# Latent attention: exponentials left in PSUM, the key sums split in two, and the value products carried over the halves

## The chip, the cores and the metric

The program runs on one core of one Trainium2 chip. The metric is the device time of one launch in microseconds (us). TensorE (PE in the profile, PEld for its weight loads) multiplies matrices into PSUM, eight banks of 128 partitions by 512 float32 numbers. VectorE (DVE) and ScalarE (ACT) read PSUM and SBUF and write either. GpSimd (POOL) works on SBUF here. All DMAs of this kernel are issued by SyncE (SP).

## The reference, cut to what matters

Two blocks run one after the other on 1024 tokens of width 1024, all in float32. The first is a pooling mixer beside an attention with a window. The second projects its normed input into a latent attention (8 heads, the part that changes), a dilated attention (24 heads in three groups), and gates, and merges them. The latent attention is a full softmax attention over all 1024 keys:

```
q = concat(q_nope, rope(q_rope)) * 96 ** -0.5        # 96 numbers a head
k = concat(k_nope, rope(k_shared))
s = einsum('bqhd,bkhd->bhqk', q, k)
p = softmax(s, axis=-1)
out = einsum('bhqk,bkhd->bqhd', p, v)                # 64 numbers a head
y_mla = (out * silu(z_mla)) @ w_o_mla
```

## The kernel before, in words

**Products in parts.** Every float32 operand of a product is split into a leading part (hi) and a rest (lo), both of the type that TensorE takes. `sub_lo` (L114, the instruction is L115) makes the rest: lo = source - hi. A projection adds three products, hi hi, hi lo and lo hi (`mm3`, L139 to L141).

**The latent attention** (L790 to L929) runs over 8 heads, each in two halves of 512 queries, each half over 8 blocks of 128 keys. For a block, three matmuls (L886 to L888) put scores as [128 keys, 512 queries] into one of three PSUM banks; a row of ones in the keys and the negated row maximum in the queries subtract the maximum. ACT takes the exponential into SBUF (`E`, L893), ACT copies its leading part (`ph`, L896), and DVE subtracts for the rest (`pl`, L898 through L115); both of its inputs lie in SBUF. Two blocks later (`LATE`) two matmuls, L880 with `ph` and L881 with `pl`, multiply by the same weights `vm`, which hold the hi and lo columns of the values side by side, and add up in one PSUM bank `o` over the half. So `o` holds the product with the values' hi on 64 partitions and with their lo on the other 64. At the end of the half all blocks still waiting are multiplied at once (L912), ACT copies one part of `o` to SBUF (L915), DVE adds the other (L916), and the sum goes to DRAM (L917).

**The denominators.** POOL adds the exponentials of the half, pair by pair (L902) and once more at the end (L920). In the next half, after block 5 (`SUMS`), `key_sums` (L832) splits that sum into hi and lo (`eh`, `el`) and multiplies both by a column of ones; a copy (L841) and a DMA bring the row to `den_d`. `finish` (L844, at heads 2, 4 and 6 and once later) takes two heads' outputs and denominators from DRAM, divides and gates them.

**The maxima of the next head.** `row_max` (L814) makes the scores of 128 queries against half of the keys from the leading parts alone (L818, one matmul into one of two banks `psT`) and DVE reduces them (L819). A head needs 16; the list `MAXES` says how many are written after each block of the head before. `max_rows` (L821) joins them, transposes them, and sends them by two DMAs (L830) into row 96 of the next head's queries; it is written after the head's last block.

**Fillers.** Projections that nothing needs until later (`fill`, 48 matmuls each, with a weight load, a split L125 and L115, and two evacuations) are written into the heads at places that `MLA_FILL` lists: 16 of them in all.

**Order.** The code is written in program order, and a planner that simulates the engines with its own costs then fixes the order of each engine's instructions. On the chip each engine runs its list in that order, and one that waits holds all that stand behind it. The planner's costs are fixed before the run.

**Banks.** `share_banks` deals out the eight PSUM banks: in this stage two for projections, three for scores, one for `o`, two for maxima, sums and transposes.

Of the kernel before, what the change touches and what calls it, by code (L numbers as in the profile page):

```python
# [19 lines left out]
# columns of the constant input (shapes alone)  # L20
# [30 lines left out]
def turn_parts():  # L51
    """1 / (2 pi) as a sum of five numbers of 12 bits."""
    from fractions import Fraction

    rest = Fraction("0.15915494309189533576888376337251436203445964574045644874766734405889679763")
    parts = []
    for _ in range(5):
        e = 0
        while rest * 2 ** e < 2 ** 11:
            e += 1  # L60
        n = int(rest * 2 ** e)
        parts.append(n * 2.0 ** -e)
        rest -= Fraction(n, 2 ** e)
    return parts
# [3 lines left out]
def hybrid_kernel(  # L68
# [21 lines left out]
    def share_banks(p, s, o, t=2):  # L90
        """The eight banks: p for projections, s for scores, o for outputs, t for transposes."""
# [37 lines left out]
    def load_w(src, n=128, kt=KT):  # L129
        """hi and lo of src, [kt * 128, n] of DRAM, as [128, kt, n]."""  # L130
        raw = raw_w()[:, :kt, :n]
        nc.sync.dma_start(raw, src.rearrange("(k p) n -> p k n", p=128))
        return split_w(raw, kt, n)

    def mm3(ps, pairs):
        """ps = sum of lhsT.T @ rhs over ((lh, ll), (rh, rl)) pairs, three products each."""
# [9 lines left out]
    def proj_half(w, h, half, kt=KT, ps=None):  # L146
        """[128, 512] of PSUM: columns of w against half of the tokens of h."""
# [11 lines left out]
    def rstd_of(ss, n):  # L159
        """(ss / n + eps) ** -0.5 of a column or several."""  # L160
# [7 lines left out]
    def norm_T(xt, gain, H, t, ahead=False):  # L168
        """Rows of xt (128 tokens), normed, times gain, transposed into H (hi, lo)."""
# [27 lines left out]
    def V_natural(vt, v):  # L197
        """vt, [2 heads x 64, tokens], to v, [tokens of a tile, tile, head, (hi | lo), 64]."""
# [9 lines left out]
    # ------------------------------------------------------------ attention of a window  # L208
    class Head:
        """Scores of 8 query tiles in [query, key] layout, probabilities, and their product  # L210
        with the values as [value (hi | lo), query].

        tiles[i] = (k0, kw, p0): keys k0 .. k0 + kw go to columns p0 .. of query tile i;
        keys[c] = [(query tile, its columns)] of the 128 keys whose values are v(c)."""
# [35 lines left out]
        def values(self, dest):  # L250
            """dest(half, top, bottom): the output is top + bottom, [64, 512] each."""
# [57 lines left out]
    # ------------------------------------------------------------ rope tables  # L309
    cs_d = tc.dram_tile([3, 32, S], F32, name="cs_d")  # L310

    def rope_tables():
        """cos, sin and -sin of position * frequency, [frequency, token]; the angle is taken
        to turns with 1 / (2 pi) in parts of 12 bits, so that each product is exact."""
# [40 lines left out]
    # ------------------------------------------------------------ first block  # L355
# [8 lines left out]
    def silu2(w, H, g):  # L364
        """2 * silu(columns of w)."""
# [14 lines left out]
    def pool_a(g):  # L380
# [18 lines left out]
        # while nothing else needs the tiles of the probabilities, they serve here too  # L399
# [7 lines left out]
    def pool_b(*gs):  # L407
        """Gates of the groups gs and their maps, half by half of the tokens."""
# [34 lines left out]
    with ExitStack() as sc:  # L443
# [12 lines left out]
        # keys: [kh; kh] and [kl; kl] of each kv head; values; queries [qh; ql] or [ql; qh]  # L456
# [18 lines left out]
        # sinks in units of unscaled scores, and the biases  # L475
# [29 lines left out]
        def normalise(hd, h):  # L505
            # 1 / (2 * (den + exp(sink - max)))
# [83 lines left out]
    # ------------------------------------------------------------ second block  # L590
# [6 lines left out]
    den_d = tc.dram_tile([8, S], F32, name="den_d")  # L597
# [14 lines left out]
    def fill_gate(j):  # L612
        """tanh((columns + bias) / 2) of one tile of the gates."""
# [6 lines left out]
    def fill_z(o, dst, j):  # L620
        """2 * silu of one tile of z."""
# [5 lines left out]
    def perm(ap, g):  # L627
        """Token order, seen as [p, residue, place] of group g."""
# [5 lines left out]
    def project_v(vt, n):  # L634
        """Values of two heads of a dilated group, with the group's order of tokens."""
# [21 lines left out]
    # projections that nothing waits for until the output, or the dilated heads  # L657
# [9 lines left out]
    # two tiles by halves, while the last tokens come  # L667
# [24 lines left out]
    MAXES = [0, 0, 1, 2, 2, 2, 2, 2, 2, 1, 1, 1, 0, 0, 0, 0]  # L692
    N_TRANS, TAIL = 1, 6
    with ExitStack() as sc:
        with ExitStack() as s2:
# [39 lines left out]
            with ExitStack() as s3:  # L735
# [12 lines left out]
                # rope of the shared keys, and a row of ones  # L748
# [6 lines left out]
                # queries: nope, and rope part * cos + swapped rope part * sin  # L755
# [13 lines left out]
            vm = vm_p.tile([128, 8, 8, 2, 64], F32R, name="vm")  # L769
# [12 lines left out]
            for t in range(8):  # L782
# [4 lines left out]
                nc.scalar.copy(vm[:, t, :, 0], p3)  # L787
                sub_lo(nc.vector, vm[:, t, :, 1], p3, vm[:, t, :, 0])
# [6 lines left out]
        def load_qk(h):  # L795
            """hi and lo of a head's [q | -max] and [k | 1]; the maxima come later."""
# [17 lines left out]
        def row_max(qk, n, i):  # L814
            """Maximum of the scores of 128 queries, from their leading parts, over half of the keys."""
# [16 lines left out]
        def key_sums(e, h, c):  # L832
# [9 lines left out]
            nc.sync.dma_start(den_d[h:h + 1, c], d)  # L842

        def finish(j):  # L844
            """Two heads over their denominators, times 2 * silu(z)."""
# [3 lines left out]
            rd = sm.tile([128, 16], F32, tag="rd2", name="rd2")  # L849
            den = den_d[2 * j:2 * j + 2].rearrange("h s -> (h s)").rearrange("(p n) -> p n", n=16)  # L850
            nc.sync.dma_start(rd, den)
# [16 lines left out]
        sums = None  # L868
        for h in range(8):
# [3 lines left out]
            for half in range(2):  # L873
                c = tokens(half)
                o = psO.tile([128, 512], F32, tag="o", name="pso")
                late, Es = [], []

                def product(kb, ph, pl, o=o, h=h):
                    v = flat(vm[:, kb, h])
                    nc.tensor.matmul(o, v, ph, start=(kb == 0), stop=False)  # L880
                    nc.tensor.matmul(o, v, pl, start=False, stop=(kb == 7))  # L881

                for kb in range(8):
# [5 lines left out]
                    if kb % 2 == 0:  # L889
                        E = P_p.tile([128, 2, 512], F32, tag="P", name="E")  # L890
                        Es.append(E)
                    e = E[:, kb % 2]
                    nc.scalar.activation(out=e, in_=ps, func=AF.Exp, scale=MSC)  # L893
                    ph = pt_p.tile([128, 512], F32R, tag="ph", name="ph")
                    pl = pt_p.tile([128, 512], F32R, tag="pl", name="pl")
                    nc.scalar.copy(ph, e)  # L896
                    sub_lo(nc.vector, pl, e, ph)
                    late.append((kb, ph, pl))  # L898
                    if len(late) > LATE:
                        product(*late.pop(0))  # L900
                    if kb % 2 and kb > 1:
                        nc.gpsimd.tensor_tensor(out=Es[0], in0=Es[0], in1=E, op=ALU.add)  # L902
# [9 lines left out]
                for item in late:  # L912
                    product(*item)
                t = ot_p.tile([128, 512], F32, tag="ot", name="ot")
                nc.scalar.copy(t[0:64], o[64:128])  # L915
                nc.vector.tensor_tensor(out=t[64:128], in0=o[0:64], in1=t[0:64], op=ALU.add)  # L916
                nc.sync.dma_start(a_d[64 * h:64 * h + 64, c], t[64:128])  # L917
                # the sum over the keys
                e = Es[0][:, 0]
                nc.gpsimd.tensor_tensor(out=e, in0=e, in1=Es[0][:, 1], op=ALU.add)  # L920
                sums = lambda e=e, h=h, c=c: key_sums(e, h, c)
            for item in ahead:
# [350 lines left out]
```

## Time and profile before

| | |
|---|---|
| median of 3 runs | 1799.38 us (1797.76 to 1809.29) |
| span of the profiled execution (first to last instruction) | 1793.0 us |
| median of the runs over that span | 6.4 us |
| PE busy | 1708.3 us, 95% |
| DVE busy | 1114.5 us, 62% |
| ACT busy | 799.0 us, 45% |
| POOL busy | 452.7 us, 25% |
| latent attention, first score to last value product | 597 to 984 us |

The profile is of one execution; its own time beyond the span is not listed, so the span stands for it. Busy time is that of instructions on an engine, as a share of the span. Matmuls overlap in the records: one of 512 columns shows some 0.39 us from start to end, while the next starts 0.23 us after it. So a stretch's count of matmuls tells more than PE's busy share: where the count is below the full pace, PE has lost time.

### The profile page before, as it was taken

The numbers are of one execution on the slowest core, as the hardware profiler recorded it, in microseconds if no ns is written. First come the engines' busy times: TensorE is split into PE (matmuls) and PEld (weight loads), VectorE is DVE, ScalarE is ACT, GpSimd is POOL, SyncE is SP. The second block draws the span as 40 slices with busy tenths as digits, with TensorE's granted clock in tenths as the row PEclk, the third lists the DMA queues.
The fourth block names the chain that finished last, engine by engine and source line by source line (L and its number), as shares of the span: only waits on it lengthen the run. The fifth ranks groups of instructions, "written<-read, shape, count | busy, mean of one in ns | idle before, by whom it ended". The sixth has DMA issues, their size and how long they took to land. (4 is left out here: it accounts for less than half of the span.)

```text
span 1793.0 us, 22070 instructions
## 1 busy us (share of the span) xinstructions
PE 1708.3 (95%) x7844; PEld 1377.0 (77%) x7844; DVE 1114.5 (62%) x1840; ACT 799.0 (45%) x1622; POOL 452.7 (25%) x287
## 2 busy tenths in 40 slices
PE   5999998999999998998989999999999999999998
PEld 4888886888787885776867778778778777877786
DVE  6787765562645577767785676775776567445432
ACT  4455433342222454555555465546545455422121
POOL 6000010011422345546554220131131122032200
PEclk9999998999999998999999999999989999999999
DMA  5211126443344221324132633463453345378542
GB/s 178 69 47 49 49 86 199 133 123 78 92 156 141 68 71 33 113 71 118 50 92 74 167 96 105 120 166 95 132 157 83 80 119 141 113 250 287 186 139 84
DMA packets 188937, 206.79 MB, mean 115 GB/s; under 512 B 29091, under 2 KB 152035, under 8 KB 188700
## 3 DMA queue, kind: packets, MB, share of 16 engines
q1 hardware_dynamic: 188828, 205.39, 39.6%
q8 instruction: 62, 1.02, 0.2%
q14 instruction: 47, 0.39, 0.1%
HBM read 126.79 MB, written 52.27 MB: 100 GB/s over the span
## 5 line engine op out<-in xcount | busy, mean ns | idle before, releaser
L139 PE MATMUL pp<-Hh,whi 128*128 128x512 f32 x1248 | 500.8, 402 | 7.2 <-ACT rt L951 4.3
L141 PE MATMUL pp<-Hh,wlo 128*128 128x512 f32 x1248 | 496.7, 398 | 0.0
L140 PE MATMUL pp<-Hl,whi 128*128 128x512 f32 x1248 | 496.2, 398 | 0.0
L139 PEld LDWEIGHTS pp<-Hh,whi 128*128 128x128 f32 x1248 | 237.8, 191 | 59.7 <-ACT rt L951 5.3
L141 PEld LDWEIGHTS pp<-Hh,wlo 128*128 128x128 f32 x1248 | 237.2, 190 | 51.6 <-issue 0.5
L140 PEld LDWEIGHTS pp<-Hl,whi 128*128 128x128 f32 x1248 | 237.4, 190 | 47.7 <-issue 0.2
L125 ACT CAST whi<-wraw 128x1024 fp32r<-128x1024 f32 (+3 forms) x110 | 109.8, 999 | 217.9 <-PE pp L140 121.8
L115 DVE TENSOR_TENSOR wlo<-wraw,whi 128x1024 fp32r<-128x1024 f32 (+3 forms) x110 | 145.4, 1323 | 93.8 <-ACT whi L125 87.3
L902 POOL TENSOR_TENSOR E<-E 128x1024 f32<-128x1024 f32 x48 | 123.5, 2573 | 208.4 <-ACT E L893 104.3
L115 DVE TENSOR_TENSOR pl<-E,ph 128x512 fp32r<-128x512 f32 x128 | 151.6, 1212 | 31.8 <-ACT ph L896 16.8
L247 ACT ACTIVATE P<-P,nm 128x256 f32<-128x256 f32 (+2 forms) x256 | 118.7, 466 | 90.3 <-DVE nm L242 90.1
L955 POOL TENSOR_TENSOR rsw<-rsw,sinT 128x1024 f32<-128x1024 f32 x24 | 72.4, 3018 | 220.8 <-DMA rsw<-rt 213.1
L819 DVE TENSOR_REDUCE mx<-pst 128x1 f32<-128x512 f32 x128 | 85.4, 683 | 60.5 <-PE pst L818 60.0
L893 ACT ACTIVATE E<-pss 128x512 f32<-128x512 f32 x128 | 74.0, 598 | 70.9 <-PE pss L888 51.3
L115 DVE TENSOR_TENSOR pl<-pst,ph 128x512 fp32r<-128x512 f32 (+2 forms) x120 | 75.5, 639 | 33.4 <-ACT ph L298 32.9
L298 ACT CAST ph<-pst 128x512 fp32r<-128x512 f32 (+2 forms) x120 | 64.4, 550 | 63.7 <-PE pst L296 58.6
L165 POOL TENSOR_TENSOR rs<-ms,mhalf 128x1 f32<-128x1 f32 (+1 forms) x40 | 25.2, 632 | 257.5 <-DVE ms L163 252.1
L896 ACT CAST ph<-E 128x512 fp32r<-128x512 f32 x128 | 76.6, 622 | 29.3 <-PE pso L880 20.2
L237 DVE CUSTOM_DVE_ANT_0 P<-pss,cc 128x256 f32<-128x256 f32 (+2 forms) x192 | 62.4, 368 | 35.3 <-PE pss L1018 24.6
L272 PE MATMUL pso<-ph,v 128*128 128x256 f32 (+1 forms) x280 | 75.4, 288 | 0.7 <-ACT ph L298 0.7
L272 PE MATMUL pso<-pl,v 128*128 128x256 f32 (+1 forms) x280 | 68.8, 283 | 3.7 <-DVE pl L115 3.7
L1018 PE MATMUL pss<-kl,qs 64*128 64x256 f32 (+2 forms) x192 | 70.4, 367 | 0.0
(266 smaller groups left out, 3199.0 us busy)
## 6 DMA issues: line engine op xcount, KB each, us to landing
wraw<-in_w_in_dram SPq DMA_DIRECT2D x78, 512.0 KB
rsw<-rt SPq DMA_DIRECT2D x96, 128.0 KB
khd<-kh SPq DMA_DIRECT2D x48, 256.0 KB
wraw<-in_w_out_dram SPq DMA_DIRECT2D x16, 512.0 KB
g_d<-g SPq DMA_DIRECT2D x16, 512.0 KB
og_d<-og SPq DMA_DIRECT2D x12, 512.0 KB
ol<-og_d SPq DMA_DIRECT2D x12, 512.0 KB
bc<-b_d SPq DMA_DIRECT2D x24, 256.0 KB
```

The lines of the kernel that those rows point to most:

```text
L115: eng.tensor_tensor(out=lo, in0=src, in1=hi.bitcast(F32), op=ALU.subtract)
L125: nc.scalar.copy(wh, raw)
L139: nc.tensor.matmul(ps, lh, rh, start=(i == 0), stop=False)
L140: nc.tensor.matmul(ps, lh, rl, start=False, stop=False)
L141: nc.tensor.matmul(ps, ll, rh, start=False, stop=(i == n - 1))
L247: nc.scalar.activation(out=a, in_=a, func=AF.Exp, bias=self.nm[:, i:i + 1], scale=self.scale, accum_out=self.den[:, i:i + 1])
L272: nc.tensor.matmul(o[b][:, q0:q0 + 128 * w], self.v(c), part[:, cols + 128 * n:cols + 128 * (n + w)], start=b not in opened, stop=(part is ...
L819: nc.vector.tensor_reduce(out=mx[:, n, i:i + 1], in_=ps, axis=mybir.AxisListType.X, op=ALU.max)
L893: nc.scalar.activation(out=e, in_=ps, func=AF.Exp, scale=MSC)
L896: nc.scalar.copy(ph, e)
L902: nc.gpsimd.tensor_tensor(out=Es[0], in0=Es[0], in1=E, op=ALU.add)
L955: nc.gpsimd.tensor_tensor(out=sw, in0=sw, in1=sinT, op=ALU.mult)
```

## The change

The exponential is written over the scores in PSUM, and the leading part and the rest are made from there. The leading part `ph` now lies in the tile `E`, and POOL adds up the leading parts alone, one block at a time (7 additions of 512 columns a half, in place of 3 of 1024 and one of 512). The rests' sum over the keys comes from TensorE: `vm` gets a 129th column of ones; the product with `ph` uses columns 0 to 127 (lo and hi of the values) into `o`, the product with `pl` uses columns 64 to 128 (hi and the ones) into a second bank `o2`, whose row 64 is the sum. Each half's evacuation then has two ACT copies, two DVE additions and two DMAs, and `finish` loads and adds two rows of denominators. The list `late` is no longer emptied at the end of a half: the last two blocks' products are written inside blocks 0 and 1 of the next half, and so is the evacuation. The maxima are spread over blocks 0 to 11 of the head, mostly one a block, and `max_rows` is written after block 4 of the second half. From the first head on, `o` has two banks and the maxima one. Comments are dropped everywhere.

```diff
-    MAXES = [0, 0, 1, 2, 2, 2, 2, 2, 2, 1, 1, 1, 0, 0, 0, 0]
+    MAXES = [1, 1, 1, 1, 1, 1, 2, 1, 1, 2, 2, 2, 0, 0, 0, 0]
...
-            vm = vm_p.tile([128, 8, 8, 2, 64], F32R, name="vm")
+            vm = vm_p.tile([128, 8, 8, 129], F32R, name="vm")
+            nc.vector.tensor_scalar(out=vm[:, :, :, 128], in0=ident[:, 0:64].rearrange("p (a b) -> p a b", a=8), scalar1=0.0, scalar2=1.0, op0=ALU.mult, op1=ALU.add)
...
-                nc.scalar.copy(vm[:, t, :, 0], p3)
-                sub_lo(nc.vector, vm[:, t, :, 1], p3, vm[:, t, :, 0])
+                nc.scalar.copy(vm[:, t, :, 64:128], p3)
+                sub_lo(nc.vector, vm[:, t, :, 0:64], p3, vm[:, t, :, 64:128])
...
-            nc.sync.dma_start(den_d[h:h + 1, c], d)
+            nc.sync.dma_start(den_d[0, h:h + 1, c], d)
...
-            rd = sm.tile([128, 16], F32, tag="rd2", name="rd2")
-            den = den_d[2 * j:2 * j + 2].rearrange("h s -> (h s)").rearrange("(p n) -> p n", n=16)
-            nc.sync.dma_start(rd, den)
+            rd2 = sm.tile([128, 2, 16], F32, tag="rd2", name="rd2")
+            for i in range(2):
+                nc.sync.dma_start(rd2[:, i], den_d[i, 2 * j:2 * j + 2].rearrange("h s -> (h s)").rearrange("(p n) -> p n", n=16))
+            rd = rd2[:, 0]
+            nc.vector.tensor_tensor(out=rd, in0=rd, in1=rd2[:, 1], op=ALU.add)
...
         sums = None
+        share_banks(2, 3, 2, 1)
+        late = []
+
+        class Half:
+            pass
+
+        def product(kb, ph, pl, H):
+            if kb == 0:
+                H.o = psO.tile([128, 512], F32, tag="o", name="pso")
+                H.o2 = psO.tile([128, 512], F32, tag="o", name="pso2")
+            nc.tensor.matmul(H.o, vm[:, kb, H.h, 0:128], ph, start=(kb == 0), stop=(kb == 7))
+            nc.tensor.matmul(H.o2[0:65], vm[:, kb, H.h, 64:129], pl, start=(kb == 0), stop=(kb == 7))
+            if kb < 7:
+                return
+            t = ot_p.tile([128, 512], F32, tag="ot", name="ot")
+            u = ot_p.tile([128, 512], F32, tag="ot", name="ou")
+            nc.scalar.copy(t[0:64], H.o[64:128])
+            nc.vector.tensor_tensor(out=t[0:64], in0=H.o[0:64], in1=t[0:64], op=ALU.add)
+            nc.scalar.copy(u[0:65], H.o2[0:65])
+            nc.vector.tensor_tensor(out=t[0:64], in0=t[0:64], in1=u[0:64], op=ALU.add)
+            nc.sync.dma_start(a_d[64 * H.h:64 * H.h + 64, H.c], t[0:64])
+            nc.sync.dma_start(den_d[1, H.h:H.h + 1, H.c], u[64:65])
...
-                o = psO.tile([128, 512], F32, tag="o", name="pso")
-                late, Es = [], []
-                def product(kb, ph, pl, o=o, h=h):
-                    v = flat(vm[:, kb, h])
-                    nc.tensor.matmul(o, v, ph, start=(kb == 0), stop=False)
-                    nc.tensor.matmul(o, v, pl, start=False, stop=(kb == 7))
+                H = Half()
+                H.h, H.c = h, c
+                acc = None
...
                     if kb % 2 == 0:
-                        E = P_p.tile([128, 2, 512], F32, tag="P", name="E")
-                        Es.append(E)
-                    e = E[:, kb % 2]
-                    nc.scalar.activation(out=e, in_=ps, func=AF.Exp, scale=MSC)
-                    ph = pt_p.tile([128, 512], F32R, tag="ph", name="ph")
+                        E = P_p.tile([128, 2, 512], F32R, tag="P", name="E")
+                    ph = E[:, kb % 2]
                     pl = pt_p.tile([128, 512], F32R, tag="pl", name="pl")
-                    nc.scalar.copy(ph, e)
-                    sub_lo(nc.vector, pl, e, ph)
-                    late.append((kb, ph, pl))
+                    nc.scalar.activation(out=ps, in_=ps, func=AF.Exp, scale=MSC)
+                    nc.scalar.copy(ph, ps)
+                    sub_lo(nc.vector, pl, ps, ph)
+                    late.append((kb, ph, pl, H))
...
-                    if kb % 2 and kb > 1:
-                        nc.gpsimd.tensor_tensor(out=Es[0], in0=Es[0], in1=E, op=ALU.add)
+                    if kb == 1:
+                        acc = pt_p.tile([128, 512], F32, tag="ph", name="acc")
+                        nc.gpsimd.tensor_tensor(out=acc, in0=E[:, 0].bitcast(F32), in1=E[:, 1].bitcast(F32), op=ALU.add)
+                    elif kb > 1:
+                        nc.gpsimd.tensor_tensor(out=acc, in0=acc, in1=ph.bitcast(F32), op=ALU.add)
...
-                for item in late:
-                    product(*item)
-                t = ot_p.tile([128, 512], F32, tag="ot", name="ot")
-                nc.scalar.copy(t[0:64], o[64:128])
-                nc.vector.tensor_tensor(out=t[64:128], in0=o[0:64], in1=t[0:64], op=ALU.add)
-                nc.sync.dma_start(a_d[64 * h:64 * h + 64, c], t[64:128])
-                e = Es[0][:, 0]
-                nc.gpsimd.tensor_tensor(out=e, in0=e, in1=Es[0][:, 1], op=ALU.add)
-                sums = lambda e=e, h=h, c=c: key_sums(e, h, c)
-            for item in ahead:
-                row_max(nxt, *item)
-            if nxt:
-                max_rows(nxt)
+                    if (half, kb) == (1, 4) and nxt:
+                        max_rows(nxt)
+                sums = lambda e=acc, h=h, c=c: key_sums(e, h, c)
             qk = nxt
+        while late:
+            product(*late.pop(0))
         sums()
```

## Rows read from the trace of the kernel before

**Rows 1.** Stretches: length, PE, PEld, DVE, ACT, POOL busy us (instructions); clock, DMA share, GB/s

```profile
685.00:735.00 50.00, 40.81 (x129) 26.73 (x128) 42.38 (x46) 22.91 (x43) 23.49 (x11) 0.80 0.20 52
...
690.00:700.00 10.00, 6.34 (x11) 2.55 (x12) 7.54 (x13) 1.43 (x3) 0.24 (x1) 0.54 0.28 67
...
805.00:835.00 30.00, 24.80 (x98) 17.25 (x97) 29.19 (x32) 18.40 (x35) 19.95 (x9) 1.00 0.32 83
905.00:930.00 25.00, 19.73 (x77) 13.31 (x76) 24.19 (x29) 16.26 (x32) 16.18 (x7) 1.00 0.19 49
...
840.00:880.00 40.00, 40.00 (x174) 32.32 (x173) 26.83 (x31) 22.20 (x39) 18.94 (x9) 1.00 0.31 92
```

**Rows 2.** DVE's groups in the three stretches in turn: busy us, mean ns, idle before

```profile
L115 DVE TENSOR_TENSOR pl<-E,ph 128x512 fp32r<-128x512 f32 x18 | 24.7, 1401 | 3.0 <-ACT ph L896 2.1 <-PE pso L881 0.9
...
L115 DVE TENSOR_TENSOR pl<-E,ph 128x512 fp32r<-128x512 f32 x15 | 17.6, 1201 | 0.0
...
L115 DVE TENSOR_TENSOR pl<-E,ph 128x512 fp32r<-128x512 f32 x14 | 14.8, 1082 | 0.0
```

**Rows 3.** The rest's subtraction: ns min/median/max, latent attention, then dilated

```profile
L115 DVE TENSOR_TENSOR pl<-E,ph x128: 674/691/2902, 599.9 to 983.3; 128x512 fp32r<-128x512 f32 x128
...
L115 DVE TENSOR_TENSOR pl<-pst,ph x88: 271/683/694, 1027.2 to 1561.1; 128x512 fp32r<-128x512 f32 x72, 128x384 fp32r<-128x384 f32 x8, 128x128 fp32r<-128x128 f32 x8
```

**Rows 4.** Timeline inside the first stretch: start us, duration us, engine, instruction

```profile
705.92 9.67 DVE L115 TENSOR_TENSOR pl<-E,ph 128x512 fp32r<-128x512 f32 x5
...
706.75 8.29 POOL L902 TENSOR_TENSOR E<-E 128x1024 f32<-128x1024 f32 x3 [16.50 <-DVE pl L115]
```

**Rows 5.** Timeline, the end of head 1

```profile
697.49 0.27 ACT L827 ACTIVATE mt<-pst 8x128 fp32r<-8x128 f32 x1 [1.48 <-DMA den_d<-den]
697.78 0.68 SPq L830 DMA_DIRECT2D qh<-mt  x1
...
699.68 0.74 PE L886 MATMUL pss<-qh,kh 97*128 97x512 f32 x1
```

**Rows 6.** Groups by line: busy us, mean ns, idle before it and its releasers

```profile
L902 POOL TENSOR_TENSOR E<-E 128x1024 f32<-128x1024 f32 x48 | 123.5, 2573 | 208.4 <-ACT E L893 104.3
L819 DVE TENSOR_REDUCE mx<-pst 128x1 f32<-128x512 f32 x128 | 85.4, 683 | 60.5 <-PE pst L818 60.0
L893 ACT ACTIVATE E<-pss 128x512 f32<-128x512 f32 x128 | 74.0, 598 | 70.9 <-PE pss L888 51.3
L896 ACT CAST ph<-E 128x512 fp32r<-128x512 f32 x128 | 76.6, 622 | 29.3 <-PE pso L880 20.2
...
L915 ACT COPY ot<-pso 64x512 f32<-64x512 f32 x16 | 9.3, 584 | 1.7 <-PE pso L881 1.4
L916 DVE TENSOR_TENSOR ot<-pso,ot 64x512 f32<-64x512 f32 x16 | 10.9, 684 | 17.3 <-ACT ot L915 17.0
```

**Rows 7.** Single lines: ns min/median/max, first and last start

```profile
L920 POOL TENSOR_TENSOR E<-E x16: 1305/1629/1748, 613.9 to 976.7; 128x512 f32<-128x512 f32 x16
...
L115 DVE TENSOR_TENSOR el<-E,eh x16: 674/1719/3367, 634.8 to 985.0; 128x512 fp32r<-128x512 f32 x16
...
L838 PEld LDWEIGHTS psd<-eh,ones x16: 79/82/126, 637.4 to 984.1; 128*1 128x1 f32 x16
...
L880 PEld LDWEIGHTS pso<-ph,vm x128: 186/188/330, 604.2 to 983.5; 128*128 128x128 f32 x128
...
L842 SPq DMA_DIRECT2D den_d<-den x16: 221/236/448, 639.4 to 993.7; - x16
```

**Rows 8.** Who waited for whom, 590 to 990: us in total, times, longest

```profile
PEld pso L881 <- DVE pl L115: 18.7, 21, 2.2
...
PEld pst L818 <- DVE mx L819: 7.6, 11, 1.8
...
PE pst L818 <- DVE mx L819: 3.6, 5, 1.3
...
PE pso L880 <- DVE ot L916: 1.0, 3, 0.4
```

More of the change, by code (lines that the diff above doesn't have):

```diff
@@ L596, in hybrid_kernel @@
     ag_d = tc.dram_tile([512, S], F32, name="ag_d")
-    den_d = tc.dram_tile([8, S], F32, name="den_d")
+    den_d = tc.dram_tile([2, 8, S], F32, name="den_d")
     rd_d = tc.dram_tile([8, S], F32, name="rd_d")
```

## The prediction, made before the change was run

> **What bounds the kernel now.** I read the stretches first. In a dense stretch PE issues 174 matmuls in 40 us, one per 0.230 us, and loses nothing; three stretches of the latent attention fall short of that pace [rows 1]. At 685 to 735 us 129 matmuls would need 29.7 us and took 50, at 805 to 835 98 would need 22.5 and took 30, at 905 to 930 77 would need 17.7 and took 25. That is 20.3, 7.5 and 7.3 us lost, 35.1 in all. The change has as many matmuls as before (five a block, 16 maxima a head, two sums a half), so 35.1 us is also about the most that it can give; nothing outside this stage is touched, and I let the rest follow earlier by what is won here.
>
> The same rows say who is full there: DVE, 29.2 of 30 us and 24.2 of 25. DVE's groups show with what: the subtraction for the rest, at a mean of 1401, 1201 and 1082 ns [rows 2]. By itself it takes 0.69 us; the maximum is 2902 [rows 3]. The timeline shows what it meets: five of them take 9.67 us while POOL adds exponentials for 8.29 [rows 4]. Both engines have two inputs in SBUF there. In the dilated attention the same subtraction takes its source from PSUM and only the leading part from SBUF. Of 88, some under POOL's work too, none took over 694 ns [rows 3]. So POOL does not slow that form.
>
> In the first stretch something is added: the end of head 1. The negated maxima of head 2 leave ACT at 697.49, after a wait for a denominator's DMA, their own DMA is issued at 697.78, and head 2's scores start at 699.68 [rows 5]. Between 690 and 700 PE got 11 matmuls through; the mean granted clock was 0.54, near the lower of its two levels (1.2 of 2.4 GHz), after PE had been waiting for `pl` and for the maxima [rows 1].
>
> **The change, part by part.**
>
> *The subtraction from PSUM.* It should take 0.684 us wherever it stands. DVE's need in the stretches falls by 18 x (1.401 - 0.684) = 12.9, 15 x (1.201 - 0.684) = 7.8 and 14 x (1.082 - 0.684) = 5.6 us. The Trainium skill, Perfetto Trace Analysis, section Optimizing Scalar/DVE Operations, speaks against this: DVE's access overhead is some 60 ns on SBUF and 125 on PSUM, so each subtraction would pay 65 ns more, an estimate of 3 us over these 47. The trace does not agree: the medians, in which POOL plays no part, are 691 from SBUF and 683 from PSUM [rows 3].
>
> *The evacuation.* Each half gets a second ACT copy (0.584), and a second DVE addition with both inputs in SBUF [rows 6]. Alone I price that addition as L916, 0.68; the nearest contended form, `el`, has a median of 1.72 [rows 7]. Two such fall into the first stretch, one into each other. DVE then needs 42.4 - 12.9 + (1.4 to 3.4) = 30.9 to 32.9 us; 29.2 - 7.8 + (0.7 to 1.7) = 22.1 to 23.1; 24.2 - 5.6 + (0.7 to 1.7) = 19.3 to 20.3. Against PE's 29.7, 22.5 and 17.7 the larger need sets each stretch: 30.9 to 32.9, 22.5 to 23.1, 19.3 to 20.3. Won: 17.1 to 19.1, 6.9 to 7.5, 4.7 to 5.7, together 28.7 to 32.3; I take 30.5. The first of these asks that the head boundary's stall goes too.
>
> *The head boundary.* `max_rows` moves four blocks forward, past the last blocks' scores and products, with its two DMAs on SP. Four blocks are 4 x 6 x 0.230 = 5.5 us even without a filler; from the maxima's copy to the scores it took 2.2 [rows 5]. So it is covered if DVE keeps up, and the products that wait for the last `pl` no longer stand before the boundary. If DVE is late, the scores wait for the maxima again.
>
> *ACT.* The exponential's destination in PSUM is not in the trace. I bound it by ACT's own range on 512 columns, 0.58 to 0.62, and take today's 598 ns. The leading part read from PSUM should take 584 (L915) to 622 (as now) [rows 6]. In 805 to 835 ACT is busy 18.4 of 30 us [rows 1]; with 0.6 more it stays under PE's 22.5. If DVE were no bound, ACT would be next: two passes a block, 1.2 us, against PE's 6 x 0.230 = 1.38.
>
> *POOL.* 16 x 7 additions at 1.31 to 1.63 us are 146 to 183 us [rows 7], against 123.5 us in rows of 1024 columns [rows 6] and 26 in the 16 last ones. POOL idled 208 us before the former, so this costs nothing; what waits for it, the sum at block 5 of the next half, has five blocks of cover.
>
> *TensorE's weights.* A load of 65 columns lies between one column's 82 ns and 128 columns' 188 [rows 7], under the pace of 230: nothing. The ones column, one strided DVE write ahead of the stage, has the dense stretch before the first head as cover. On SP, 16 more issues of 0.24 us [rows 7] and four small loads wait for `u` or for `den_d`; behind them stand weight loads, several of which are ahead. Nothing. Four additions of 16 columns in `finish`: under 1 us of DVE.
>
> *New waits.* (a) One bank for maxima: a maximum's matmul now waits for the reduction before it, and scores and products stand behind it on PE. With two banks it waited 16 times, 11.2 us [rows 8]. Bounds: nothing, up to a whole reduction of 0.683 for each of the 112 inside the heads, 76 us. Since the maxima now come one a block instead of two, and DVE is less late, I take 5. (b) Across the halves: between the last product and the first of the next half only a block's three scores and one maximum are written, 0.9 us, while the first bank needs copy and addition, 1.27. Bounds: nothing where a filler lies between (waits for this were 1.0 us in 3 [rows 8]), and 0.35 x 15 = 5.3; I take 2.5. (c) A score bank is now held by the copy and the subtraction as well: 0.7 + 0.6 + 0.6 + 0.7 = 2.6 us, while three banks last 3 x 1.38 = 4.1. I take 0, with 1.5 us of lateness of DVE as the point where scores begin to wait.
>
> **Sum.** 30.5 - 5 - 2.5 = 23 us off the profiled span of 1793.0: 1770. The median of the runs stands 6.4 above that span; with the same offset, 1776.4. I say 1776.
>
> **The rivals.**
>
> *B: only the boundary goes.* The fillerless stretches stay as slow, since DVE, ACT and PE are then all nearly full (23, 19 and 22.5 us in the second) and wait for one another through the score banks. The 10 us around the boundary, in which 11 matmuls needed 2.5, give some 7.5; with a little of the rest, 8 to 13 us: 1787 to 1791. For it: DVE's need still exceeds PE's in the third stretch. Against it: today's waits there name `pl`, 21 times on the weight loads [rows 8].
>
> *C: slower, by the single bank of the maxima.* PE stands still at L818 until L819 is done. The cycle is 0.4 for the matmul, 0.68 for the reduction and 0.68 for a subtraction ahead of it on DVE, 1.76 us against 1.38 of PE work a block. It decides once more than 30.5 / 0.683 = 45 of the 112 wait for a whole reduction; at 75 of them 51 - 30.5 = 21 us are lost: 1820. For it: 16 waits even with two banks. Against it: in stretches with fillers a block has 2.8 us, and the planner can put matmuls between.
>
> *D: the contention stays.* If POOL slowed the subtraction through its SBUF input alone, DVE would gain nothing and have the second addition on top: the boundary's 7.5 less 3, 1795. Against it stand the 88 subtractions [rows 3].
>
> **How the numbers follow.** Forecast 0.60, B 0.25, C 0.11, D 0.04. A change of about 1%, 18 us, can be told from none. The forecast's own gain runs from 12 (both new waits doubled and a little more) to 35, 1764 to 1787, and some nine tenths of it lie over 18 us: faster 0.54. Same: B, D and the forecast's lower end, 0.35. Slower: C, 0.11. The range takes in the most that can be won, 1764, and B and D, up to 1795, with 3 and 5 us beyond for the order that the planner chooses elsewhere, 1761 to 1800; it leaves out C.
>
> **What would show it.** In the profile after: the subtraction at 0.68 us with a maximum near its mean; POOL's additions at 1.3; no scores waiting for `qh`'s DMA; matmuls per stretch near the full pace throughout the stage. It would be wrong if L818 waited tens of times for L819 (C), if the fillerless stretches kept their gaps with ACT or the score banks named (B), or if the planner, with new costs, put the fillers elsewhere and left new stretches without them.

## The result, and the profile after

The changed kernel takes 1844.13 us (median of 4 runs, 1841.69 to 1848.12) against 1798.57 for the kernel before on the same chip (median of 4, one run more than the three listed ahead of the change): 1.0251 times as long, interval 1.0221 to 1.0282. It is 2.5% slower, where 1776 us was forecast, and lies above the range's 1800. Its direction is that of rival C, slower by the single bank of the maxima, to which the prediction gave a chance of 0.11 and 1820 us.

The profiled span grew from 1793.0 to 1841.7 us, 48.7. Here is the stage from its first score to its last value product (length; then busy us and instructions of PE, PEld, DVE, ACT and POOL; granted clock, DMA share, GB/s), the kernel before first:

```profile
597.20:984.40 387.20, 367.26 (x1515) 282.45 (x1513) 283.70 (x301) 209.84 (x366) 198.52 (x86) 0.97 0.27 77
```

and the same stage of the changed kernel:

```profile
592.30:1029.70 437.40, 400.13 (x1557) 290.27 (x1555) 216.78 (x315) 221.70 (x386) 188.88 (x131) 0.93 0.25 71
```

The stage is 50.2 us longer. It holds 42 matmuls more, which are other work that before stood ahead of the stage; at 0.230 us they are 9.7 us, and the stage begins 4.9 us earlier. What is left over the full pace rose from 387.2 - 1515 x 0.230 = 38.8 us to 437.4 - 1557 x 0.230 = 79.3. DVE, which the forecast took for the bound, has 67 us less to do, and that has not helped.

The groups of the changed kernel (busy us, mean ns, idle before it and what ended it) show each operation at about its forecast price; L821, L820, L115 and L917 answer to L819, L818, L898 and L893 of the kernel before [rows 3, 6, 8]:

```profile
L821 DVE TENSOR_REDUCE mx<-pst 128x1 f32<-128x512 f32 x128 | 87.2, 685 | 108.7 <-PE pst L820 108.5
L928 POOL TENSOR_TENSOR acc<-acc,E 128x512 f32<-128x512 f32 x96 | 127.7, 1330 | 61.5 <-ACT E L918 57.8
...
L115 DVE TENSOR_TENSOR pl<-pss,E 128x512 fp32r<-128x512 f32 x128 | 85.4, 685 | 52.4 <-ACT E L918 43.1
L917 ACT ACTIVATE pss<-pss 128x512 f32<-128x512 f32 x128 | 74.6, 586 | 66.9 <-PE pss L912 66.3
...
L820 PE MATMUL pst<-kh,qh 96*128 96x512 f32 x128 | 59.2, 465 | 17.6 <-DVE mx L821 16.8
L918 ACT CAST E<-pss 128x512 fp32r<-128x512 f32 x128 | 74.1, 590 | 3.4
```

The first row points at the loop: DVE idled 108.7 us before a maximum's reduction, waiting for its matmul (60.5 in [rows 6]). That alone costs nothing, since DVE has less to do. The waits of the stage (us in total, times, longest) have the other half, the matmul that waits for the reduction:

```profile
DVE mx L821 <- PE pst L820: 92.1, 59, 4.8
...
PEld pst L820 <- DVE mx L821: 27.9, 28, 2.4
...
PE pst L820 <- DVE mx L821: 16.3, 21, 2.0
...
PEld pso L886 <- DVE pl L115: 11.2, 27, 0.5
...
PEld pss L910 <- DVE pl L115: 8.6, 11, 1.4
...
PE pso L885 <- DVE ot L892: 3.8, 5, 0.9
...
PE pss L910 <- DVE pl L115: 3.6, 5, 0.9
```

One wait can show in two rows, on the weight load (PEld) and on the matmul behind it (PE). All 21 on L820's matmul are among the 28 on its weight load, so the two rows are not added. L820 waited 28 times for L821, 27.9 us on the weight load; before it was 11 times and 7.6 [rows 8]. The wait for the rest `pl`, TensorE's largest before (18.7), is down to 11.2.

Now where this falls. Four stretches of the changed kernel (columns as in [rows 1]):

```profile
672.00:710.00 38.00, 29.73 (x97) 18.41 (x96) 18.80 (x29) 16.51 (x29) 16.15 (x11) 0.80 0.07 18
...
795.00:823.00 28.00, 21.12 (x66) 10.84 (x65) 18.14 (x29) 14.71 (x27) 17.04 (x12) 0.85 0.02 5
909.00:940.00 31.00, 22.92 (x67) 12.56 (x65) 18.09 (x30) 14.88 (x26) 16.16 (x11) 0.74 0.09 22
...
755.00:785.00 30.00, 30.00 (x134) 24.38 (x133) 6.35 (x9) 6.64 (x11) 0.00 (x0) 1.00 0.30 88
```

The first three are the second halves of heads 1, 3 and 5. The second and third hold no filler, the first only the end of one, 28 matmuls up to 682.4: 38 - 97 x 0.230 = 15.7, 12.8 and 15.6 us lost, 44.1 together. In [rows 1] DVE was busy 42.4 of 50 us; here it is busy 18.8 of 38, and no engine is full. Such a stretch is not bound by anybody's work but by a chain. The fourth has the full pace, full clock and hardly any maxima: the fillers stand there, one behind another. Over the whole stage four stretches are without a filler's matmul (from 682, 787, 906 and 1004 us on), 567 matmuls in 210 us. That is 79 us over the full pace, so practically all that the stage loses is lost there.

The maxima are crowded into the stretches without fillers. DVE's group in the 42 us ahead of the first stretch, which are full of fillers, and in that stretch (630 to 672, then 672 to 710):

```profile
L821 DVE TENSOR_REDUCE mx<-pst 128x1 f32<-128x512 f32 x6 | 4.1, 686 | 4.4 <-PE pst L820 4.4
...
L821 DVE TENSOR_REDUCE mx<-pst 128x1 f32<-128x512 f32 x13 | 8.9, 687 | 6.4 <-PE pst L820 6.4
```

And the timeline at the end of head 1 (start us, duration, engine, instruction, idle before it and what ended it; weight loads left out) shows the chain itself:

```profile
700.41 0.69 DVE L821 TENSOR_REDUCE mx<-pst 128x1 f32<-128x512 f32 x1 [0.89 <-PE pst L820]
701.16 0.80 PE L820 MATMUL pst<-kh,qh 96*128 96x512 f32 x1 [0.78 <-DVE mx L821]
...
701.99 0.69 DVE L821 TENSOR_REDUCE mx<-pst 128x1 f32<-128x512 f32 x1 [0.89 <-PE pst L820]
702.74 0.79 PE L820 MATMUL pst<-kh,qh 96*128 96x512 f32 x1 [0.78 <-DVE mx L821]
703.57 0.69 DVE L821 TENSOR_REDUCE mx<-pst 128x1 f32<-128x512 f32 x1 [0.88 <-PE pst L820]
704.31 0.80 PE L820 MATMUL pst<-kh,qh 96*128 96x512 f32 x1 [0.78 <-DVE mx L821]
705.14 0.69 DVE L821 TENSOR_REDUCE mx<-pst 128x1 f32<-128x512 f32 x1 [0.89 <-PE pst L820]
...
706.09 0.37 PE L827 MATMUL pst<-cc,mx 128*8 128x128 f32 x1 [0.99 <-DVE mx L825]
706.50 0.27 ACT L829 ACTIVATE mt<-pst 8x128 fp32r<-8x128 f32 x1 [8.30 <-PE pst L827]
706.80 0.69 SPq L832 DMA_DIRECT2D qh<-mt  x1
...
708.64 1.65 PE L910 MATMUL pss<-qh,kh 97*128 97x512 f32 x3 [0.49 <-DMA qh<-mt]
```

Matmul, reduction, matmul, reduction: one maximum every 1.58 us, and each engine idles for about as long as the other works. PE's list holds nothing else there: head 1's products stand before it, and head 2's scores need these maxima. The stretch around it, in the columns of [rows 1]:

```profile
700.00:706.00 6.00, 2.76 (x4) 0.86 (x3) 2.90 (x5) 0.00 (x0) 2.62 (x2) 0.50 0.00 0
```

Four matmuls in 6 us, and a granted clock of 0.50, the lower level (1.2 of 2.4 GHz), after PE had waited before one matmul after another; a maximum's matmul shows 0.80 us there, against 0.39 at the full clock, which lengthens the chain again.

### The profile page after: what moved, and what is told of

It reads as the page before. It is cut to its first block, busy times and chain, and to the rows that moved or that the text cites. A ratio compares the mean times of both kernels' runs of the same rounds, so it can differ in the third digit from the quotient of the medians.

```text
span 1841.7 us, 22270 instructions
## 1 busy us (share of the span) xinstructions
PE 1735.3 (94%) x7844; PEld 1379.1 (75%) x7844; DVE 1045.5 (57%) x1861; ACT 807.4 (44%) x1638; POOL 442.6 (24%) x335
## 4 chain that ended last, share of the span: by engine, by line
PE 51%; DVE 6%; DMA 6%; ACT 5%; issue 3%; SPq 2%; POOL 1%; DVEq 0%; POOLq 0%; ACTq 0%
PE pp L139 10%; PE pp L141 9%; PE pp L140 9%; PE pss L1035 2%; PE pso L272 2%; DMA bc<-b_d 2%; PE pss L1034 2%; PE pst L820 2%; PE y L139 2%; PE y L141 2%; PE y L140 2%; PE pss L910 1%; PE pso L886 1%; PE pss L912 1%; PE pss L911 1%
## 5 line engine op out<-in xcount | busy, mean ns | idle before, releaser
L141 PEld LDWEIGHTS pp<-Hh,wlo 128*128 128x128 f32 x1248 | 237.3, 190 | 50.2 <-issue 0.3
L115 DVE TENSOR_TENSOR wlo<-wraw,whi 128x1024 fp32r<-128x1024 f32 (+3 forms) x110 | 139.3, 1267 | 111.7 <-ACT whi L125 106.0
L821 DVE TENSOR_REDUCE mx<-pst 128x1 f32<-128x512 f32 x128 | 87.2, 685 | 108.7 <-PE pst L820 108.5
L928 POOL TENSOR_TENSOR acc<-acc,E 128x512 f32<-128x512 f32 x96 | 127.7, 1330 | 61.5 <-ACT E L918 57.8
L115 DVE TENSOR_TENSOR pl<-pss,E 128x512 fp32r<-128x512 f32 x128 | 85.4, 685 | 52.4 <-ACT E L918 43.1
L917 ACT ACTIVATE pss<-pss 128x512 f32<-128x512 f32 x128 | 74.6, 586 | 66.9 <-PE pss L912 66.3
L115 DVE TENSOR_TENSOR pl<-pst,ph 128x512 fp32r<-128x512 f32 (+2 forms) x120 | 75.6, 639 | 33.5 <-ACT ph L298 32.9
L820 PE MATMUL pst<-kh,qh 96*128 96x512 f32 x128 | 59.2, 465 | 17.6 <-DVE mx L821 16.8
L918 ACT CAST E<-pss 128x512 fp32r<-128x512 f32 x128 | 74.1, 590 | 3.4
```

Of the source, the lines that this page charges most:

```text
L115: eng.tensor_tensor(out=lo, in0=src, in1=hi.bitcast(F32), op=ALU.subtract)
L141: nc.tensor.matmul(ps, ll, rh, start=False, stop=(i == n - 1))
L820: nc.tensor.matmul(ps, q[0][0:96, 128 * i:128 * i + 128], k[0][0:96, tokens(n)], start=True, stop=True)
L821: nc.vector.tensor_reduce(out=mx[:, n, i:i + 1], in_=ps, axis=mybir.AxisListType.X, op=ALU.max)
L917: nc.scalar.activation(out=ps, in_=ps, func=AF.Exp, scale=MSC)
L918: nc.scalar.copy(ph, ps)
```

## The experiments

All are timed against the kernel before in the same series; the ratios have their 95% interval. `share_banks(a, b, c, d)` deals banks to projections, scores, `o` and maxima.

**The one bank alone, in the kernel before.**

```diff
         sums = None
+        share_banks(2, 3, 1, 1)
```

> The kernel before, with one bank instead of two for the maxima from the first head on (the bank left over is unused). Theory 1 (the single bank makes each row maximum wait for the reduction before it, and the chain is left uncovered at the ends of heads): 30 to 45 us slower than before, 1830 to 1845, with L818 waiting for L819 some 40 to 60 times. Theory 2 (the order of the new list of maxima, the products across the halves, or score banks held longer cost the time): within 5 us of before, about 1800.

Measured: 1912.36 us, 1.0629 [1.0584, 1.0674]. That is 113 us slower than the kernel before, more than either theory had. So one bank is enough for a loss of this size. The waits show why it is dearer here:

```profile
PEld pso L882 <- DVE pl L115: 48.0, 32, 3.6
PE pso L882 <- DVE pl L115: 33.4, 24, 3.2
...
PEld pst L818 <- DVE mx L819: 27.1, 29, 1.8
PE pst L818 <- DVE mx L819: 13.7, 21, 1.1
```

L818 waits 29 times, fewer than the 40 to 60 that were expected, 27.1 us on the weight load, about as in the changed kernel. But the subtraction still has both inputs in SBUF and takes up to 2902 ns as in [rows 3], and the products wait 48.0 us in 32 for it, against 18.7 in 21 with two banks [rows 8].

**Dealing banks a second time.** As above, with the numbers left as they were: `share_banks(2, 3, 1)`.

> The kernel before, with its banks dealt a second time after the first head's maxima, the same (2, 3, 1, 2). The changed kernel lost some 5 us more than before ahead of its first score. If dealing banks there costs it: 3 to 8 us slower than before, 1802 to 1807. If it is the single bank or the changed order: within 2 us of before.

Measured: 1797.68 us, 0.999 [0.9959, 1.002]. The second deal costs nothing that can be told from the spread of the runs; that leaves the number of banks.

**A second bank for the maxima in the changed kernel**, taken from the projections, and in another run from the scores.

```diff
-        share_banks(2, 3, 2, 1)
+        share_banks(1, 3, 2, 2)
```

> The changed kernel, with two banks for the maxima and one for projections in this stage (1, 3, 2, 2). Theory 1: the chain of maxima is short again and the subtraction's gain appears, 1775 to 1795, unless fillers now wait for their one bank (then up to 1810). Theory 2: as the changed kernel, 1835 to 1850.

```diff
-        share_banks(2, 3, 2, 1)
+        share_banks(2, 2, 2, 2)
```

> The changed kernel, with two banks for the maxima and two for scores (2, 2, 2, 2). Theory 1: 1780 to 1800; the score banks are held about 2.6 us a block, two of them last 2.8, so some waits of scores for the subtraction appear. Theory 2 with the score banks as the cause: slower than the changed kernel, over 1850.

Measured: 1789.06 us, 0.9937 [0.9911, 0.9963], and 1805.46, 1.0042 [1.0016, 1.0068]. Either way most of the loss is gone: 56 us by the difference of the ratios (0.0314 x 1798) with one bank for the projections, 38 with two for the scores. The first lies in the range of theory 1, the second 5 us above it; there the bank is missed elsewhere, and the scores wait for the subtraction, as was expected:

```profile
PEld pss L910 <- DVE pl L115: 18.8, 41, 1.2
```

**The second bank, dealt from the start.** The changed kernel with one projection bank from before the first head's maxima on:

```diff
-        share_banks(2, 3, 1)
+        share_banks(1, 3, 2, 2)
...
-        share_banks(2, 3, 2, 1)
```

> The changed kernel with banks (1, 3, 2, 2) dealt once at the stage's start, instead of (2, 3, 1, 2) and a second deal after the first head's maxima. The kernel with (1, 3, 2, 2) dealt second measured 1789 and lost some 15 us before its first score. If that loss comes from the second deal: 1773 to 1780. If it comes from one bank for projections: 1786 to 1795.

Measured: 1782.14 us, 0.9924 [0.9903, 0.9944]. This is the whole computation of the change, and it is faster than both kernels, by 10 to 17 us against the one before. It falls between the two outcomes that were thought possible, and its ratio can't be told from 0.9937, so what the second deal cost here stays open. The stage and its wait:

```profile
566.70:952.70 386.00, 378.75 (x1596) 290.99 (x1595) 227.36 (x322) 219.72 (x390) 194.76 (x131) 0.99 0.29 85
```

```profile
PEld pst L820 <- DVE mx L821: 2.1, 3, 1.6
```

1596 matmuls in 386 us leave 18.9 us over the full pace, against 79.3, and the clock is 0.99.

**Three banks shared by projections, maxima and sums.**

```diff
-        share_banks(2, 3, 1)
+        share_banks(3, 3, 2, 0)
...
-            ps = psT.tile([128, 512], F32, tag="t", name="pst")
+            ps = pp.tile([128, 512], F32, tag="pp", name="pst")
...
```

> The changed kernel with banks (3, 3, 2) dealt once: maxima, sums and transposes share three banks with the projections, no bank of their own. Theory 1: a maximum can take any of three banks, 1770 to 1790. Rival (a projection holds its bank for 24 matmuls, so the maxima wait for banks as they do now): 1800 or slower.

Measured: 1807.99 us, 1.0058 [1.0017, 1.0098]. Better than one bank for the maxima and worse than two, and in the rival's range. Lines are one further down in this kernel. A maximum's matmul hardly waits for a reduction any more (1.9 us in 8), but the maxima of some heads still come late; where they are joined the transposition waits:

```profile
PEld pst L828 <- DVE mx L826: 12.1, 5, 3.8
...
PE pst L828 <- DVE mx L826: 9.9, 5, 3.4
```

That is the smaller part of its loss. The first score comes at 583.3, 14 us earlier than in the kernel before, with 163 projection matmuls fewer ahead of it, which are 37 us of work; so some 24 us are lost ahead of the stage. What loses them was not followed.

**Exponentials in PSUM**, with the leading parts in `E` and POOL adding them one block at a time, in the kernel before, and no other part of the change:

```diff
-                    e = E[:, kb % 2]
-                    nc.scalar.activation(out=e, in_=ps, func=AF.Exp, scale=MSC)
-                    nc.scalar.copy(ph, e)
-                    sub_lo(nc.vector, pl, e, ph)
+                    ph = E[:, kb % 2]
+                    nc.scalar.activation(out=ps, in_=ps, func=AF.Exp, scale=MSC)
+                    nc.scalar.copy(ph, ps)
+                    sub_lo(nc.vector, pl, ps, ph)
...
```

> The kernel before with only the exponentials kept in PSUM, the leading parts in E and POOL adding them one block at a time; two banks for maxima, one for outputs, the old list of maxima, products emptied at each half's end. Left out: the rests are not in the denominators. Theory 1: the subtraction's gain alone, 15 to 25 us faster than before, 1775 to 1785. Theory 2 with the score banks held longer as the cause: slower than before, 1810 or more.

Measured: 1789.83 us, 0.995 [0.9926, 0.9974]. The part that was to bring most brings 9 us (5 to 13), not 15 to 25.

**The same with one bank** (`share_banks(2, 3, 1, 1)` added).

> The kernel before with the exponentials kept in PSUM (as in the run that measured 1790) and one bank for the maxima; the old list of maxima, products emptied at each half's end, one bank for outputs. Left out: the rests are not in the denominators. With one bank the kernel before took 1912, the changed kernel 1844, and undoing the spread list or the run-on products left that at 1842. If the subtraction from PSUM alone makes the single bank cheaper, 1835 to 1850. If the second output bank or all the parts together are needed for it, 1870 or more.

Measured: 1837.28 us, 1.0235 [1.0216, 1.0254]. Against the run without that line 0.0285 x 1797 = 51 us (the intervals together: 6 either way). This is the price of one bank where nothing else in the program differs and the subtraction is short. Against one bank in the kernel before (1.0629) the short subtraction is worth 71 us (0.0394 x 1798, 9 either way), where with two banks it is worth 9. L818's waits are here

```profile
PEld pst L818 <- DVE mx L819: 22.5, 29, 1.3
...
PE pst L818 <- DVE mx L819: 10.6, 15, 0.8
```

The order of PE's list differs as well. In stretches of more than 6 us without a filler's matmul stand 350 of the stage's matmuls with two banks and 602 with one, and what is lost over the full pace in them is 30 and 71 us.

**The change with two banks for the maxima and one for the output** (both products go into `o`, so the second evacuation is gone):

```diff
...
-        share_banks(2, 3, 2, 1)
...
-            nc.tensor.matmul(H.o2[0:65], vm[:, kb, H.h, 64:129], pl, start=(kb == 0), stop=(kb == 7))
+            nc.tensor.matmul(H.o, vm[:, kb, H.h, 0:128], pl, start=False, stop=(kb == 7))
...
```

> The changed kernel without its second output bank, so that maxima keep two banks and projections two: both products go to one bank by all 128 columns, as before; the spread list of maxima, the early joining of the maxima and the products across the halves stay. Left out: the rests are not in the denominators. Theory 1 (the only harm is the single bank): in the stage the losses fall below 12 us from 38, 1770 to 1778. Rival (the early maxima or the products across the halves do harm of their own): 1790 or slower, no better than the subtraction from PSUM alone (1790).

Measured: 1777.75 us, 0.9904 [0.9866, 0.9942]. Between this and the changed kernel lie 0.0347 x 1798 = 62 us, for the one bank and the second output bank's work together.

**That kernel, with `late` emptied at each half's end.**

```diff
+                while late:
+                    product(*late.pop(0))
                 sums = lambda e=acc, h=h, c=c: key_sums(e, h, c)
```

> The run with two banks for maxima and one for outputs that measured 1778, with the products emptied at each half's end again; the spread list and the early joining of the maxima stay. Left out: the rests are not in the denominators. If the early joining is what gave 12 us over the subtraction from PSUM alone (1790): 1775 to 1781. If the products across the halves gave it: 1787 to 1793.

Measured: 1775.1 us, 0.9885 [0.9863, 0.9907]. Products that run on across the halves bring nothing that can be told from none (the ratios differ by 0.0019, 0.0044 either way). Against the exponentials in PSUM alone this kernel has only the spread list and the early join, apart from the layout of `vm`: 0.0065 x 1797 = 12 us (6 either way). Its stage (to a microsecond), and DVE at the end of head 1:

```profile
598.00:964.00 366.00, 359.50 (x1510) 281.31 (x1508) 209.38 (x301) 212.28 (x369) 189.69 (x134) 0.99 0.28 81
```

```profile
687.57 1.95 DVE L821 TENSOR_REDUCE mx<-pst 128x1 f32<-128x512 f32 x3
...
689.88 2.34 POOL L115 TENSOR_TENSOR ql<-rawq,qh 96x1024 fp32r<-96x1024 f32 x1
690.03 2.21 DVE L825 TENSOR_TENSOR mx<-mx 128x8 f32<-128x8 f32 x1
```

With two banks three reductions run back to back in 1.95 us; with one, the last three in the changed kernel's timeline take 3.85 from the first one's start to the third one's end, at the lower clock. The stage is left with 366.0 - 1510 x 0.230 = 18.7 us over the full pace.

**The run-on alone, and the order of the maxima alone, in the changed kernel.** First `late` emptied as above; then the old list and join:

> The changed kernel with the list of waiting products emptied at each half's end, as before; one bank for maxima as changed. The kernel before with one bank took 1912, the changed kernel 1844, and the old list of maxima in the changed kernel 1842. If the products that run on are what makes the single bank cheaper in the changed kernel (they leave PE work beside the chain of maxima): 1870 to 1900. If it is the subtraction from PSUM, which frees DVE for the reductions: within 10 us of the changed kernel, 1835 to 1855.

```diff
-    MAXES = [1, 1, 1, 1, 1, 1, 2, 1, 1, 2, 2, 2, 0, 0, 0, 0]
+    MAXES = [0, 0, 1, 2, 2, 2, 2, 2, 2, 1, 1, 1, 0, 0, 0, 0]
...
-                    if (half, kb) == (1, 4) and nxt:
-                        max_rows(nxt)
...
+            for item in ahead:
+                row_max(nxt, *item)
+            if nxt:
+                max_rows(nxt)
```

> The changed kernel with the old list of maxima and the old place for joining them (end of the head); one bank for maxima as changed. Theory 1: the chain of 16 maxima starts later and ends after the head's last products, so more of it is uncovered: between the changed kernel and the old kernel with one bank, 1860 to 1895. Rival (the spread list is what upset the order): faster than the changed kernel, under 1835.

Measured: 1842.06 us, 1.0256 [1.0231, 1.028], and 1841.76, 1.0259 [1.0218, 1.03]. Both are the changed kernel's time. The slower outcomes that were thought possible did not come: under one bank neither edit matters in either direction. The loop stands in both traces (L820 waits 29 and 26 times, 27.6 and 19.4 us on the weight load). That the maxima are late whatever the program's order asks for is the likely reason; no run shows it by itself.

## Why the prediction was wrong, point by point

**Right.** *The subtraction from PSUM*: 0.684 us forecast, 0.685 measured. Its own row in the changed kernel (ns min/median/max) beside [rows 3], where the maximum was 2902:

```profile
L115 DVE TENSOR_TENSOR pl<-pss,E x128: 616/691/694, 594.5 to 1028.6; 128x512 fp32r<-128x512 f32 x128
```

So rival D is out. *POOL*: 1330 ns an addition, at the low end of 1.31 to 1.63. *ACT*: the exponential into PSUM 586 ns, the copy from it 590, inside 0.58 to 0.62. *TensorE's weights*: the 65-column load, between 82 and 188 ns as said:

```profile
L886 PEld LDWEIGHTS pso<-pl,vm x128: 133/137/228, 599.5 to 1029.3; 128*65 128x65 f32 x128
```

*New wait (b)*, across the halves: L885 waited 3.8 us in 5, taken at 2.5. *New wait (c)*, score banks: L910 waited 8.6 us in 11 for the subtraction, on the weight load, taken at 0 with DVE's lateness as the condition; a small miss. *The head boundary* was not covered: scores still waited for the DMA of the maxima (L910 for `qh`, 4.2 us in 3), though DVE had time to spare.

**The step that failed** is term (a) of the sum, "Since the maxima now come one a block instead of two, and DVE is less late, I take 5", between bounds of 0 and 76. Measured, one bank costs 51 us where it is the only difference in the program, 56 by giving the changed kernel its second bank. The value was taken near the wrong bound for two reasons. I read the waits of a kernel with two banks and scaled them down, but there the second bank lets PE write the next maximum while DVE reduces the last, so those rows cannot show what happens without it. (The 16 waits and 11.2 us were misread too: two rows of the same waits were added, and there are 11, of 7.6 us.) And I let the program's list say when the maxima run. In the trace 6 of them stand in 42 us full of fillers and 13 in the next 38, whose fillers end after 10; the list was replaced with no effect.

**Rival C named the loop, and undersized what comes with it.** Its loop was 1.76 us a maximum and 75 waits, 51 us; measured are 1.58 us where nothing stands between, and 28 waits, 27.9 us on the weight load, 20 more than before. Tens of such waits were the prediction's own sign for C. But the stage loses 79.3 - 18.9 = 60.4 us more than the whole computation with two banks, so the waits alone are not the loss. Counted from one matmul's start to the next, over 0.230 us each, 25.6 of the 79.3 us stand ahead of the 28 matmuls that waited for a reduction (1.3 with two banks). Another 15.1 stand at 76 matmuls that waited for nothing but were issued at a granted clock under 0.9 (3.9 with two banks). The rest stands mostly ahead of matmuls that waited for `pl`, for the score and output banks, for the sums and for the joins, in the stretches without fillers. C had no place for these.

**The gain was smaller than said, too.** With two banks the sum would have been 28 us. The nearest kernels, without the second evacuation, gained 0.0096 x 1799 = 17 and 0.0115 x 1797 = 21; the complete one with a projection bank less, 14. Rival B, only the boundary goes, would have been 8 to 13; what was measured is 9 for the subtraction and 12 for the early join and the spread list, so neither part alone. Each stretch was priced by the larger of DVE's and PE's own work, as if neither waited for the other; with two banks the stage still loses 18.7 us.

**Open.** How the cost of one bank divides between the waiting itself and the order that the planner fixes for it. With the exponentials in PSUM, where only the bank differs, 602 matmuls stand without fillers in place of 350. At the loss a matmul of the kernel with two banks (30 us over 350) the 602 would lose 52, so by this estimate about half of the 41 us between 30 and 71 is the order. No run here held the order while the banks changed. The five us that the changed kernel loses ahead of the stage did not come with the second deal alone (0.999); what they are was not settled.

## What to carry to other kernels

A bank between a matmul and a reduction is a buffer of a loop: with two, the dearer of both sets the pace, with one their sum does, and no row of a kernel that has two shows that sum, so it must be added up from the two durations and their signals (here 1.58 us at the lower clock, against 0.65 for each of three back to back) and compared with the work that can really stand beside it. Before giving up a bank, look for the stretch in which nothing else is left for the engines, and price the loop there, not on the average. Where a planner fixes the order, expect it to move with the number of banks. When an engine that was the bound gets cheaper, look at what else runs in a loop through it.

## What the runs showed of the hardware

DVE can be held until POOL's instruction ends, however small its own work. In the last timeline above, a maximum of 8 elements a partition, both inputs in SBUF, took 2.21 us: it ended at 692.24, when POOL's subtraction (689.88 + 2.34 = 692.22) ended. The same instruction took 0.17 us in the changed kernel:

```profile
705.87 0.17 DVE L825 TENSOR_TENSOR mx<-mx 128x8 f32<-128x8 f32 x1
```

With the second bank dealt from the start it met two of POOL's instructions in a row, took 4.73 us, and ended at 671.07, again with POOL's last (671.04):

```profile
665.69 3.00 POOL L115 TENSOR_TENSOR kl<-rawk,kh 96x1024 fp32r<-96x1024 f32 x1 [4.64 <-ACT kh L810]
666.34 4.73 DVE L825 TENSOR_TENSOR mx<-mx 128x8 f32<-128x8 f32 x1
668.65 2.39 POOL L115 TENSOR_TENSOR ql<-rawq,qh 96x1024 fp32r<-96x1024 f32 x1
```

The Trainium skill, SBUF — State Buffer, section Who interferes with whom, says that the two share a pair of ports under an exclusive lock, and that a DVE instruction with two SBUF inputs contends with a GpSimd instruction that reads SBUF. The trace agrees, in these rows and in the subtraction: with one input moved to PSUM, its worst case went from 2902 to 694 ns while POOL's additions went from 64 to 112, shorter ones.

The Trainium skill, Perfetto Trace Analysis, section Optimizing Scalar/DVE Operations, gives DVE an access overhead of some 60 ns on SBUF and 125 on PSUM, which by an estimate makes each subtraction from PSUM 65 ns dearer. The trace does not agree: the median is 691 ns from either.
